# A macaron FFN turned to token-major products with 512 moving features

## The chip, the cores and the metric

The kernel runs on one core of one Trainium2 chip. The metric is the device time of one execution in microseconds. The core has a matrix engine (TensorE, PE in the profile, with its weight loads shown apart as PEld), VectorE (DVE), ScalarE (ACT), GpSimd (POOL) and SyncE (SP). SP and POOL issue most of the DMAs, each from a queue that is worked off in order. Matmul results accumulate in PSUM, which has eight banks of 128 x 512 float32.

## The reference

One encoder block on 512 tokens of 1024 features, all in float32:

```
x = x + 1/2 * (silu(g) * u) @ W_down          g, u = halves of RMSNorm(x) @ W_gu   (FFN 1)
x = x + (sigmoid(gA)*A + sigmoid(gB)*B) @ W_out      A: conv and two RG-LRU scans, B: neighbourhood attention
x = x + 1/2 * (silu(g) * u) @ W_down          with its own weights                 (FFN 2)
```

The FFN is 2816 wide, that is 22 tiles of 128 features; W_gu is 1024 x 5632, W_down 2816 x 1024. The RMSNorm's gain is multiplied into x before the product; its factor for each token (rstd, r) is applied behind the product.

## The kernel before

**Three matmuls for one.** Float32 accuracy is reached with a faster number format: every operand is cut into a high part H and a low part L (`split`, L143: a ScalarE copy that rounds, then a VectorE subtraction), and each product is H·H + H·L + L·H, three matmuls (`mm3`, L171). A weight tile of 128 x 1024 is loaded into `wraw` by SP, split into `wh` and `wl` (four buffers of each), and used.

**Features on the partitions.** x lies with features on the 128 partitions and the 512 tokens along the free axis, eight tiles. A matmul in which the weights are stationary and x moves gives features x tokens.

**FFN, gate and up.** Some feature tiles are computed plainly (`chunk`, 24 matmuls of 512 columns for a tile of g or of u); their number is NPLAIN, 4 in FFN 1 and 0 in FFN 2. The others go two at a time through `strassen` (L294), a Strassen scheme with seven products where eight would be needed. Its 2 x 2 split runs over the two halves of the features going in, the two halves of the tokens, and g against u. The x side are sums and differences of quarters of x (`a11`, `a12`, `a22` and the forms `s1` to `s4`, built once per FFN by `make_forms`); the weight side are sums that are partly built by DMAs from POOL that add into the loaded tile (`add`, L358), partly by VectorE (`after_sum`, L362). A product (`product`, L302) is 24 matmuls with 256 tokens moving: 2 feature tiles x 4 k-tiles x 3. The order in a unit is a11, a12, s1, a22 of the unit before, s2, s4, s3. Results are copied out of PSUM by ScalarE (`p1`, `p5`, `u2`), VectorE adds to them, multiplies the gate by r (L332), ScalarE takes the Silu (L333), VectorE multiplies by u (`put`, L339). h stays in SBUF, features on the partitions.

**The beginnings.** FFN 1 begins with x and the first NLEAD = 6 weight chunks arriving in pieces: for each of the eight k-tiles six chunks x 3 matmuls are done as soon as the tile is there (L464 to L468). VectorE and ScalarE make xh, xl, the sum of squares and the forms from the same tiles meanwhile. In FFN 2 two units' a11 come first, and the sum of squares is turned into r by matmuls placed by hand between products (`late`).

**FFN, down.** Two passes over the 22 h tiles (q = 0, 1), each for four of the eight output tiles in four PSUM banks; every h tile is split in each pass. The last DTAIL = 3 pairs of h are done bank by bank, so that outputs leave one after another. An output is scaled by -0.5 r (L545) and added to x (L642 in FFN 1, L1130 in FFN 2). `out1` also prepares the next stage's xh, xl and sum of squares. The last tile of the kernel is finished in two token halves over the last EHALF = 5 tiles.

**Order of work.** The program is written in one sequence; the framework's planner puts each engine's instructions in an order from priorities (program order, raised by `high_priority`), a model of durations and free buffers. `after` adds an order without a wait, and `hold` (L251) places an instruction behind the last matmul written so far.

**Token-major elsewhere.** The qkv projection (`tok_group`, L831 to L833) has slices of x stationary and 512 weight columns moving, so that its results have tokens on the partitions.

Of the kernel before, what the change touches and what calls it, by code (L numbers as in the profile page):

```python
# [16 lines left out]
P = 128  # L17
# [32 lines left out]
NLEAD = 6  # L50


NPLAIN = 4, 0
# [3 lines left out]
EHALF = 5  # L57
# [34 lines left out]
def block_kernel(ctx: ExitStack, tc, a, out):  # L92
# [19 lines left out]
    NBIG = 43  # L112
# [181 lines left out]
    def strassen(src, units, A, r, hs, ahead, late=None):  # L294

        half = T // 2
        prev = {}

        line, in_line = [], late is not None
        view = lambda t: t.rearrange("p (m t) -> p m t", m=2)  # L300

        def product(ps, w, form, first, last):  # L302
            H, L = w
            for m in range(2):
                o = ps[:, m * half : (m + 1) * half]
                for k in range(4):
                    c = slice((m * 4 + k) * P, (m * 4 + k + 1) * P)
                    xh_, xl_ = A[form][k]


                    for w_, x_ in ((H, xh_), (H, xl_), (L, xh_)):
                        mm = nc.tensor.matmul(  # L312
                            o, w_[:, c], x_, start=first and m + k == 0 and w_ is H and x_ is xh_,
                            stop=m + k == 4 and w_ is L, skip_group_check=True)
                        if line:
                            after(mm, line.pop())
            if in_line:
                line.append(mm)

        def operand(raw, form=None):  # L320

            w = hl_t()
            with tc.high_priority():
                lo = split(raw, *w)
            if form is not None:
                after(lo, mark["cut", form])
            return w

        def gate(t, tok):
            rr = r[:, tok].unsqueeze(1).to_broadcast([P, 2, half])  # L330
            s_ = big_t(n="s")
            nc.vector.tensor_tensor(view(s_), view(t), rr, ALU.mult)  # L332
            nc.scalar.activation(s_, s_, AF.Silu)  # L333
            return s_

        def put(u, s_, t, tok):
            for m in range(2):
                c = slice(m * half, (m + 1) * half)
                mark["h"] = nc.vector.tensor_tensor(hs[u * 2 + m][:, tok], s_[:, c], t[:, c], ALU.mult)  # L339

        def last_product(p):
            product(p["Z"], p["w"](), "a22", False, True)
            put(p["u"], gate(p["Z"], slice(half, T)), p["u7"], slice(half, T))

        def begin(u):

            a_ = raw_t()
            nc.sync.dma_start(a_, src[u, 0])
            Z = acc_t()
            product(Z, operand(a_), "a11", True, False)  # L350
            p1 = big_t(n="p1")
            with tc.high_priority():
                nc.scalar.activation(p1, Z, AF.Copy)
            return a_, Z, p1

        def add(u, t, i):
            with tc.high_priority():
                nc.gpsimd.dma_start(t, src[u, i], accum_op=ALU.add)  # L358

        def after_sum(t, o, form=None):  # L360
            with tc.high_priority():
                i = nc.vector.tensor_tensor(t, t, o, ALU.add)  # L362
            if form is not None:
                after(i, mark["cut", "s1"])
            return operand(t, form)

        def behind(u, form):
            return form if late is not None and u == 0 else None

        begun = {u: begin(u) for u in range(2)} if late is not None else {}  # L370
        first = set(begun)
        for u in range(units):
            a_, Z, p1 = begun.pop(u) if u in begun else begin(u)


            b_ = raw_t()
            d = pair_t().rearrange("p a b -> p (a b)")
            c = pair_t().rearrange("p a b -> p (a b)")
            in_line = late is not None and u < 2
            soon = u == 0 or u in first  # L380
            if soon:
                add(u, a_, 1)
            for t, i in ((d, 1), (b_, 3), (c, 2)):
                nc.sync.dma_start(t, src[u, i])
            X, Y = acc_t(), aux_t()
            hs += [big_t(n="h") for _ in range(2)]
            last = u == units - 1

            def gate1():
                product(Y, w_c, "a12", True, True)  # L390
                nc.vector.tensor_tensor(p1, p1, Y, ALU.add)
                return None if u == 0 and late is not None else gate(p1, slice(0, half))

            w_c = operand(c)
            if not last:
                s1 = gate1()
            w = operand(a_) if soon else after_sum(a_, d)
            add(u, d, 3)
            product(X, w, "s1", True, False)
            p5 = big_t(n="p5")  # L400
            nc.scalar.activation(p5, X, AF.Copy)
            if prev:
                last_product(prev)
            w = after_sum(a_, b_, behind(u, "s2"))
            add(u, a_, 2)
            product(Z, w, "s2", False, False)
            u2 = big_t(n="u2")
            nc.scalar.activation(u2, Z, AF.Copy)
            if u == 0 and late is not None:
                rcol = late[0](line[-1])  # L410
            product(X, operand(b_, behind(u, "s4")), "s4", False, True)
            nc.vector.tensor_tensor(u2, u2, X, ALU.add)
            product(Z, operand(d, behind(u, "s3")), "s3", False, False)
            nc.vector.tensor_tensor(p5, p5, Z, ALU.add)
            if u == 0 and late is not None:
                late[1](rcol, line[-1])
                s1 = gate(p1, slice(0, half))
            if last:
                ahead()
                s1 = gate1()  # L420
            put(len(hs) // 2 - 1, s1, u2, slice(0, half))
            prev = dict(u=len(hs) // 2 - 1, Z=Z, u7=p5, w=lambda a_=a_: operand(a_))
        last_product(prev)

    def ffn(wgu, ws, wd, xh, xl, S, ssum, plain, res, emit_out, lead=None, end=None):
        hs = []
        r = None
        pre = {}
        if lead is not None:


            for i in range(NLEAD):
                pre[i] = acc_t() if i < 3 else aux_t()
            wts = [[None] * 2 for _ in range(NLEAD)]
            for k in range(KT):
# [25 lines left out]
                if k == KT - 1:  # L461
                    r = rstd(ssum, True)[0]
# [4 lines left out]
                for i in range(NLEAD):  # L467
                    nc.tensor.matmul(pre[i], w[i][2][:, s], xh[k], start=False, stop=k == KT - 1)  # L468
# [10 lines left out]
        for m in range(plain):  # L479
            pg = chunk(2 * m)  # L480
            if r is None:
                r = rstd(ssum)[0]
# [4 lines left out]
            nc.scalar.activation(s, g, AF.Silu)  # L487
            h = big_t(n="h")
# [23 lines left out]
        for q in range(2):  # L512
# [19 lines left out]
            for j in range(FT // 2):  # L532
                ws_.append(load_w(wd[q, j], 1024))
                ahead(q * FT + 2 * j + 2 + AHEAD)
                if j < FT // 2 - DTAIL:
                    for k in (2 * j, 2 * j + 1):
                        for i in range(4):
                            put_in(i, k)
# [675 lines left out]
```

## Time and profile before

| | |
|---|---|
| median of three runs (range) | 1108.18 us (1106.54 to 1108.5) |
| the profiled execution, its span | 1106.08 us, 1104.3 us |
| TensorE busy | 1097.9 us, 99% |
| VectorE, ScalarE busy | 74%, 52% |
| moved by DMA | 175.83 MB, 159 GB/s on average |

FFN 1 fills roughly the first 351 us, the mixer the time to 758 us, FFN 2 the rest. "Busy" of TensorE counts the time in which any matmul is under way; since matmuls overlap (a 512-column one shows 0.39 us from start to end), their cost is read from the distance between starts. In a row of instructions the numbers behind the bar are busy time in us and mean duration in ns, then the idle time of the engine before them and what ended it.

### The profile page before, as it was taken

Reading aid. Unit: us, or ns where it says so; the run is one execution under the profiler, and the core shown is the slowest. Engines: PE = TensorE matmul, PEld = TensorE weight load, DVE = VectorE, ACT = ScalarE, POOL = GpSimd, SP = SyncE. Lnnn points to the kernel's source line nnn. Section 1 sums busy time; section 2 is a strip of 40 time slices with the busy share of each in tenths; the row PEclk is TensorE's granted clock in tenths of the full one; section 3 lists DMA queues with packets and bytes.
Section 4 is the critical chain, followed back from the end, with each engine's and each line's share of the span. In section 5 each row is a group of like instructions: output and inputs, shape, how many; then the busy total and the mean of one; then the engine's idle time right before and its main releaser. Section 6 shows DMA issues by size and latency. Waiting matters only on the chain.

```text
span 1104.3 us, 17667 instructions
## 1 busy us (share of the span) xinstructions
PE 1097.9 (99%) x6811; PEld 972.1 (88%) x6811; DVE 812.9 (74%) x1295; ACT 579.4 (52%) x872; POOL 141.1 (13%) x243
## 2 busy tenths in 40 slices
PE   9999999999999999999999999999999999999998
PEld 7899999988888778788887888889999999998887
DVE  7877777794745686999878995759877777785542
ACT  8554544464443678876454552356645454464330
POOL 0000000000000351231335231000000000000000
PEclk9999999999999999999999999999999999999999
DMA  8566656643423585583787674477666666553421
GB/s 269 155 170 153 149 157 162 163 153 96 134 81 105 157 249 162 155 221 102 231 241 205 184 212 142 138 219 169 184 166 146 163 170 147 150 165 96 134 77 38
DMA packets 59429, 175.83 MB, mean 159 GB/s; under 512 B 9169, under 2 KB 12753, under 8 KB 59345
## 3 DMA queue, kind: packets, MB, share of 16 engines
q1 hardware_dynamic: 43136, 127.75, 35.3%
q0 software_dynamic: 15632, 46.70, 21.1%
q8 instruction: 53, 0.87, 0.3%
q10 hardware_dynamic: 576, 0.26, 0.1%
q14 instruction: 32, 0.25, 0.1%
HBM read 150.53 MB, written 15.73 MB: 151 GB/s over the span
## 4 chain that ended last, share of the span: by engine, by line
PE 99%; DVE 0%; issue 0%
PE acc L312 31%; PE acc L172 11%; PE acc L173 11%; PE acc L174 10%; PE aux L312 5%; PE acc L831 4%; PE acc L833 4%; PE acc L832 4%; PE aux L174 4%; PE aux L173 4%; PE aux L172 4%; PE aux L1013 1%; PE aux L742 1%; PE aux L950 1%; PE acc L464 1%; PE aux L464 1%
## 5 line engine op out<-in xcount | busy, mean ns | idle before, releaser
L145 ACT ACTIVATE wh<-wraw 128x1024 fp32r<-128x1024 f32 (+3 forms) x224 | 220.4, 987 | 300.9 <-issue 94.0
L148 DVE TENSOR_TENSOR wl<-wraw,wh 128x1024 fp32r<-128x1024 f32 (+3 forms) x236 | 267.1, 1136 | 100.1 <-ACT wh L145 99.0
L312 PE MATMUL acc<-s,wh 128*128 128x256 f32 x1280 | 232.2, 283 | 0.0
L312 PEld LDWEIGHTS acc<-s,wh 128*128 128x128 f32 x1280 | 199.7, 192 | 0.0
L312 PE MATMUL acc<-s,wl 128*128 128x256 f32 x640 | 181.2, 283 | 0.0
L312 PEld LDWEIGHTS acc<-s,wl 128*128 128x128 f32 x640 | 122.9, 192 | 0.0
L172 PE MATMUL acc<-xh,wh 128*128 128x512 f32 x272 | 107.5, 395 | 0.0
L173 PE MATMUL acc<-xl,wh 128*128 128x512 f32 x272 | 106.4, 391 | 0.0
L174 PE MATMUL acc<-xh,wl 128*128 128x512 f32 x272 | 106.4, 391 | 0.0
L312 PE MATMUL acc<-xl,wh 128*128 128x256 f32 x320 | 90.6, 283 | 0.0
L312 PE MATMUL acc<-xh,wl 128*128 128x256 f32 x320 | 90.6, 283 | 0.0
L312 PE MATMUL acc<-xh,wh 128*128 128x256 f32 x320 | 90.6, 283 | 0.0
L831 PE MATMUL acc<-wh,xh 128*128 128x512 f32 x192 | 75.7, 394 | 0.0
L832 PE MATMUL acc<-wh,xl 128*128 128x512 f32 x192 | 74.8, 390 | 0.0
L833 PE MATMUL acc<-wl,xh 128*128 128x512 f32 x192 | 74.8, 389 | 0.0
L148 DVE TENSOR_TENSOR hl<-h,hh 128x512 fp32r<-128x512 f32 x88 | 57.2, 686 | 21.7 <-PE aux L173 21.4
L172 PE MATMUL aux<-hh,wh 128*128 128x512 f32 (+1 forms) x181 | 69.9, 386 | 0.0
L173 PE MATMUL aux<-hl,wh 128*128 128x512 f32 (+1 forms) x181 | 69.9, 386 | 0.0
L174 PE MATMUL aux<-hh,wl 128*128 128x512 f32 (+1 forms) x181 | 69.9, 386 | 0.0
L173 PE MATMUL acc<-hl,wh 128*128 128x512 f32 (+1 forms) x176 | 68.0, 386 | 0.0
L172 PE MATMUL acc<-hh,wh 128*128 128x512 f32 (+1 forms) x176 | 68.0, 386 | 0.0
L174 PE MATMUL acc<-hh,wl 128*128 128x512 f32 (+1 forms) x176 | 68.0, 386 | 0.0
(221 smaller groups left out, 2286.9 us busy)
## 6 DMA issues: line engine op xcount, KB each, us to landing
wraw<-wqkv SPq DMA_DIRECT2D x24, 512.0 KB, 4.3
wraw<-wg SPq DMA_DIRECT2D x24, 512.0 KB, 8.9
wraw<-w1d SPq DMA_DIRECT2D x22, 512.0 KB, 3.6
wraw<-w2s SPq DMA_DIRECT2D x22, 512.0 KB
pair<-w2s SPq DMA_DIRECT2D x22, 512.0 KB, 4.4
wraw<-w2d SPq DMA_DIRECT2D x22, 512.0 KB, 3.7
wraw<-w1s SPq DMA_DIRECT2D x18, 512.0 KB, 3.4
pair<-w1s SPq DMA_DIRECT2D x18, 512.0 KB, 4.5
```

Source lines behind the costliest of these rows:

```text
L145: nc.scalar.activation(H, raw, AF.Copy)
L148: return nc.vector.tensor_tensor(L, raw, H.bitcast(F32), ALU.subtract)
L172: nc.tensor.matmul(ps, wh, xh, start=first, stop=False, skip_group_check=skip)
L173: nc.tensor.matmul(ps, wh, xl, start=False, stop=False, skip_group_check=skip)
L174: mark["mm"] = nc.tensor.matmul(ps, wl, xh, start=False, stop=last, skip_group_check=skip)
L312: mm = nc.tensor.matmul(o, w_[:, c], x_, start=first and m + k == 0 and w_ is H and x_ is xh_, stop=m + k == 4 and w_ is L, skip_group_che ...
L464: nc.tensor.matmul(pre[i], w[i][1][:, s], xh[k], start=k == 0, stop=False)
L742: prev, mm = mm, nc.tensor.matmul(ps[d][b], W[w][o, c], X[x][o], start=x == 1, stop=w + x == 0)
L831: nc.tensor.matmul(pss[j], xh[kk][:, tj], H[:, s], start=kk == 0, stop=False)
L832: nc.tensor.matmul(pss[j], xl[kk][:, tj], H[:, s], start=False, stop=False)
L833: mark["mm"] = nc.tensor.matmul(pss[j], xh[kk][:, tj], L[:, s], start=False, stop=kk == KT - 1)
L950: mm = hold(nc.tensor.matmul(ps[hp][:, cs], q_[o, n * P : (n + 1) * P], keys(k_[o]), start=k_ is kl, stop=q_ is ql))
```

## The change

Four tiles of g and u form a unit (five units in each FFN), and NPLAIN becomes 2, 2, NLEAD 4. In a product the x side is now stationary and the weights move, 512 features at a time: two token blocks x 4 k-tiles x 3 = 24 matmuls of 512 columns, on two PSUM banks. The weight tiles come in two halves (kp), which are summed and split just before they are used. Results have tokens on the partitions, so r is a number per partition and enters through the Silu's scale and a scalar operand. h is then turned: VectorE transposes 32 x 32 blocks, SP writes the result to a buffer in memory (`hd`), and POOL's queue reads it back with rearranged addresses (`fetch`), which gives features on the partitions. The down projection is one pass over 22 tiles with eight banks: the first DFIRST = 3 tiles two banks at a time, then all eight banks for each tile, then the last DTAIL = 3 bank by bank. The -0.5 moves into the addition to x; r is already in h. The hand-placed `late` work is dropped, FFN 2 starts with its four plain chunks, and some tiles change pools (NBIG 43 to 42, the LRU's cuts go to the PT pool).

```diff
-NLEAD = 6
-NPLAIN = 4, 0
+NLEAD = 4
+NPLAIN = 2, 2
 DTAIL = 3
-EHALF = 5
+DFIRST = 3
...
+    def strassen(src, units, A, rcol, hd):
...
+        def product(pss, ws, form, first, last):
+            for kp in range(2):
+                H, L = ws[kp]() if callable(ws[kp]) else ws[kp]
+                for k2 in range(2):
+                    k = kp * 2 + k2
+                    c = slice(k2 * T, (k2 + 1) * T)
                     xh_, xl_ = A[form][k]
+                    for tb in range(2):
+                        s = slice(tb * P, (tb + 1) * P)
+                        for x_, w_ in ((xh_, H), (xl_, H), (xh_, L)):
+                            mark["mm"] = nc.tensor.matmul(
+                                pss[tb], x_[:, s], w_[:, c], start=first and k == 0 and x_ is xh_ and w_ is H,
+                                stop=k == 3 and w_ is L, skip_group_check=True)
+            flush()
...
+        def gate(ts, th):
+            ss = [big_t(n="s") for _ in ts]
+            for tb, (s_, t) in enumerate(zip(ss, ts)):
+                j = th * 2 + tb
+                nc.scalar.activation(s_, t, AF.Silu, scale=rcol[:, j : j + 1])
+            return ss
+
+        def flush():
+            while out:
+                nc_dma, t2 = out.pop(0)
+                hold(nc.sync.dma_start(nc_dma, t2))
+
+        def put(u, ss, ts, th):
+            for tb, (s_, t) in enumerate(zip(ss, ts)):
+                j = th * 2 + tb
+                mark["h"] = nc.vector.scalar_tensor_tensor(t, t, rcol[:, j : j + 1], s_, ALU.mult, ALU.mult)
+                t2 = big_t(n="ht")
+                nc.vector.transpose(
+                    t2.rearrange("p (c f i) -> p f c i", c=NCB, i=32), t.rearrange("p (f c i) -> p f c i", c=NCB, i=32))
+                out.append((hd[u][j], t2.rearrange("p (c x) -> p c x", c=NCB)))
...
         for u in range(units):
+            a_ = raws(u, 0, "pair", 4)
+            c_ = raws(u, 2, "PT", 5)
+            d_ = raws(u, 1, "PT", 5)
+            b_ = raws(u, 3, "wraw", 3)
+            Z = [acc_t() for _ in range(2)]
+            product(Z, operands(a_), "a11", True, False)
+            p1 = evict(Z, "p1")
+            if u == 0:
                 add(u, a_, 1)
...
+        def fetch(u):
+            for th in range(2):
+                t = big.tile([P, 8, NCB, 32], F32, tag="PT", bufs=5, name=nm("hT"))
+                for c in range(NCB):
+                    hold(nc.gpsimd.dma_start(
+                        t[c * 32 : (c + 1) * 32].rearrange("p g f i -> p g (f i)"),
+                        hd[u].rearrange("t (a i) c x -> c i (t a) x", a=NCB)[c][:, th * 8 : th * 8 + 8]))
+                turned[u, th] = t
...
+        for g in range(4):
+            outs = range(2 * g, 2 * g + 2)
+            for m in outs:
+                ps[m] = (aux_t, acc_t)[g % 2]()
+            for k in first:
+                for m in outs:
+                    put_in(m, k)
+        for k in range(DFIRST, FT):
+            ws_[k] = load_w(wd[k], 1024)
+            ahead(k + 1 + AHEAD)
+            if k < FT - DTAIL:
+                for m in range(KT):
+                    put_in(m, k, FT - 1 - DTAIL if end is not None and m == KT - 1 else FT - 1)
...
+        for m in range(KT):
+            if end is not None and m == KT - 1:
+                break
+            for k in range(FT - DTAIL, FT):
+                put_in(m, k)
+            emit_out(m, ps[m])
...
-        nc.vector.tensor_tensor(xres[m], ps, xres[m], ALU.add)
+        nc.vector.scalar_tensor_tensor(xres[m], ps, -0.5, xres[m], ALU.mult, ALU.add)
```

More of the change, by code (lines that the diff above doesn't have):

```diff
@@ L371, in strassen @@
-        first = set(begun)
-        for u in range(units):
[L373 to L381, printed above, removed]
-                add(u, a_, 1)
[L383 to L398, printed above, removed]
+                split(raw, *w)
@@ L409, in strassen @@
[L409 to L420, printed above, removed]
```

255 lines of the change are left out of this document (121 added, 134 removed).

## The prediction

> **What bounds the kernel now.** I read the page first: its first part for the engines, its fourth for the chain that ended last.
>
> ```profile
> span 1104.3 us, 17667 instructions
> PE 1097.9 (99%) x6811; PEld 972.1 (88%) x6811; DVE 812.9 (74%) x1295; ACT 579.4 (52%) x872; POOL 141.1 (13%) x243
> ...
> PEclk9999999999999999999999999999999999999999
> ...
> PE 99%; DVE 0%; issue 0%
> ```
>
> TensorE is busy from end to end at its full clock, and the chain is TensorE alone: a microsecond is won only by a shorter stream of matmuls, and lost wherever that stream now has to wait. A busy PE can still hide a slow pace, so I next read the chain in order of time, in which a piece of n matmuls lasts n times the distance from start to start. First the gate-and-up products of FFN 1, then the qkv projection, then the opening.
>
> ```profile
> 73.44 17.28 PE acc L312 x144
> ...
> 471.84 0.23 PE acc L831
> ...
> 480.00 0.23 PE acc L831
> ...
> 13.60 0.68 PE acc L464 x3
> ...
> 17.68 0.68 PE acc L464 x3
> ```
>
> In L312 a 256-column matmul starts every 17.28/144 = 120.0 ns. L831 to L833 are already what the change makes of L312, x stationary and 512 weight columns moving: from 471.84 to 480.00 there are 36 of them, 8.16/36 = 226.7 ns. Two narrow ones cost 240.0, one wide one 226.7. The opening spends 4.08 us on each 128 rows of x (18 wide matmuls), also without a gap.
>
> Last I looked at how near the other engines are to the end of their slack, by stretches (PE, PEld, DVE, ACT, POOL, clock, DMA): opening, seven products of FFN 1, down projection of FFN 1, and the start of FFN 2.
>
> ```profile
> 0.00:32.45 32.45, 31.39 (x136) 25.97 (x137) 25.53 (x59) 25.20 (x46) 2.68 (x12) 1.00 0.84 270
> 72.00:232.00 160.00, 160.00 (x1335) 159.96 (x1334) 121.70 (x146) 80.94 (x100) 12.81 (x15) 1.00 0.64 161
> 232.00:330.00 98.00, 98.00 (x434) 81.15 (x433) 61.99 (x104) 47.38 (x70) 0.00 (x0) 1.00 0.35 109
> 760.00:780.00 20.00, 20.00 (x170) 20.00 (x169) 18.09 (x26) 14.45 (x21) 1.70 (x2) 1.00 0.65 178
> ```
>
> VectorE is the second engine: 76% in the products, 79% in the opening, 90% where FFN 2 starts.
>
> **Seven products, 512 wide.** Before: 9 + 11 units of two feature tiles, each 7 x 24 matmuls, 3360 in all at 120.0 ns = 403.2 us. After: 5 + 5 units of four tiles, 1680 at 226.7 ns = 380.8 us. Gain 22.4 us. The plain tiles go from 4 + 0 to 2 + 2, the same number at the same width, so they add nothing.
>
> By the Trainium skill, "TensorE: Matmul & The Clock Gate", section on the 56 ns gap, back-to-back matmuls start N cycles of 2.4 GHz plus about 2.5 ns apart. Then a pair would save only 2.5 ns and the whole 4.2 us. The trace does not agree: 120.0 and 226.7 are 13.3 ns above N/2.4 in both widths, so the pairing saves 13.3, not 2.5.
>
> **VectorE and ScalarE beside it.** The rows of 72 to 232 us (eight units, that is four of the new size), and the nearest rows for what is new:
>
> ```profile
> L148 DVE TENSOR_TENSOR wl<-wraw,wh 128x1024 fp32r<-128x1024 f32 x41 | 50.1, 1222 | 14.8 <-ACT wh L145 14.8
> L148 DVE TENSOR_TENSOR wl<-pair,wh 128x1024 fp32r<-128x1024 f32 x15 | 18.3, 1222 | 9.2 <-ACT wh L145 9.2
> L362 DVE TENSOR_TENSOR wraw<-wraw,wraw 128x1024 f32<-128x1024 f32 x7 | 8.5, 1220 | 0.0
> L339 DVE TENSOR_TENSOR h<-s,u 128x256 f32<-128x256 f32 x16 | 6.7, 423 | 0.2
> L332 DVE TENSOR_TENSOR s<-acc,rstd 128x512 f32<-128x512 f32 x8 | 5.5, 692 | 5.1 <-PE acc L312 5.1
> L391 DVE TENSOR_TENSOR p<-p,aux 128x512 f32<-128x512 f32 x8 | 5.5, 688 | 5.4 <-PE aux L312 5.4
> ...
> L992 DVE STREAM_TRANSPOSE pt<-p 128x512 f32<-128x512 f32 x16 | 10.9, 684 | 0.0
> ...
> L856 DVE TENSOR_SCALAR v<-acc,rcol 128x512 f32<-128x512 f32 x8 | 5.8, 746 | 0.1
> ```
>
> Per four tiles before: 14 splits x 1.22 + 4 sums x 1.22 + 6 adds x 0.69 + 4 scalings by rstd x 0.69 + 8 half products x 0.42 = 32.2 us of 40.3. After: splits, sums and adds the same (26.1); the scaling goes into the Silu's per-row scale on ScalarE; four products with a per-row scalar (0.75, the L856 row) and four 32x32 transposes (0.68): 31.8 us of 38.1, 83%. ScalarE keeps its instructions. Four weight buffers still hold two products, 10.9 us, ahead of TensorE, so I price this at nothing; if VectorE runs out of cover it is the third rival.
>
> **h through memory.** A unit adds four writes of 256 KB on SP's queue, each behind its transpose and placed after the following product's last matmul, and eight reads of 128 KB (512-byte pieces) on POOL's queue, placed after the last product. Nearest rows, issue by issue with the median time to landing:
>
> ```profile
> PT<-pd POOLq DMA_DIRECT2D x64, 112.0 KB, 4.1
> ...
> wraw<-w1s POOLq DMA_DIRECT2D x10, 512.0 KB, 5.8
> ...
> xd<-pair SPq DMA_DIRECT2D x16, 256.0 KB, 2.3
> ```
>
> About 1 MB more per 38.1 us is 27 GB/s on top of the products' 161, which the faster pace makes 170; 270 were moved in the opening. SP's next weight loads stand behind those writes, but the transposes end about 4 us after their product and the write's place is a product (5.44 us) later. The reads stand behind the accumulating loads, the last of which leaves after s2 of the last unit, three products (16.3 us) before the down projection. Unit 0 of h is then there in time; units 1 to 4 are fetched four k-steps (21.8 us) before use. Nothing, unless the hand-over below is late.
>
> **Hand-over from products to down projection (twice).** The down projection now starts with k = 0, 1 (plain tiles) and 2 (unit 0). The cut of k = 2 stands in VectorE's queue behind the last unit's last gate: two Silu (1.2), two products and two transposes (2.9), then the cut in halves (1.2 with ScalarE's half): about 5.5 us after the last product. Its first pair of banks needs it after 12 matmuls, 2.7 us. If the planner lets the next pairs' k = 0, 1 go first, nothing waits; if not, 2.8 us. I take 0.75 each time, 1.5 in all (0 to 5.6).
>
> **Down projection.** As many matmuls. Per k-step of 24 x 226.7 ns = 5.44 us VectorE has one split and two half cuts, 1.22 + 0.84; each h is cut once, not twice. Cheaper beside the path, zero on it. At the end of FFN 1 the eight outputs come 2.04 us apart (three k-steps a bank), where four came 4.08 apart:
>
> ```profile
> 347.51 0.69 DVE L545 SCALAR_TENSOR_TENSOR dn<-acc,rstd 128x512 f32<-128x512 f32 x1 [0.52 <-PE acc L174]
> 348.23 0.69 DVE L642 TENSOR_TENSOR pair<-dn,pair 128x512 f32<-128x512 f32 x1
> ...
> 349.76 0.75 DVE L197 SCALAR_TENSOR_TENSOR xl<-pair,small,xh 128x512 fp32r<-128x512 f32 x1 [0.19 <-ACT xh L196]
> 350.43 0.69 DVE L206 TENSOR_TENSOR ssum<-ssum,xsq 128x512 f32<-128x512 f32 x1
> ```
>
> One of the first two goes, so an output costs VectorE 0.7 + 0.7 + 0.7 = 2.1 us: it just keeps pace. The mixer's first chunk needs x's last tile 21 matmuls (4.8 us) after the last output; a backlog of two outputs would make that late. I take 0.5 (0 to 3).
>
> **The opening of FFN 1.** Here cover goes. With four early chunks instead of six TensorE wants a new 128 rows every 12 x 0.2267 = 2.72 us, while x's part of the work on VectorE and ScalarE is unchanged. VectorE's rows up to the last xl (31.79 + 0.75):
>
> ```profile
> 31.79 0.75 DVE L197 SCALAR_TENSOR_TENSOR xl<-pair,small,xh 128x512 fp32r<-128x512 f32 x1
> ...
> L148 DVE TENSOR_TENSOR wl<-wraw,wh 128x512 fp32r<-128x512 f32 x6 | 3.7, 684 | 0.0
> L148 DVE TENSOR_TENSOR wl<-wraw,wh 128x1024 fp32r<-128x1024 f32 x3 | 3.7, 1221 | 0.0
> L148 DVE TENSOR_TENSOR wl<-wraw,wh 128x256 fp32r<-128x256 f32 x6 | 2.3, 419 | 0.1
> ```
>
> Of 25.5 us busy, a third of the six lead weights' rows goes (3.3 of 10.0, with the smaller pieces) and the three 1024-wide splits (3.7); 6.9 us are idle, mostly before the first data. 18.5 + 6.9 = 25.4 us, plus up to four urgent splits for a11 and a12 (4.9): 25.4 to 30.3. TensorE wants that tile at 4.8 + 7 x 2.72 + 0.9 = 24.8. So it waits 0.6 to 5.5 us. After that, s1's forms and weights, the late rows and the two plain gates, some 14 us of VectorE, stand against the 13.5 us up to s1: another 0 to 2. ScalarE (25.2 busy) and the DMAs (4.2 MB at 270 GB/s, 15.5 us) are close behind. I take 4.5 (0.6 to 9). FFN 2 gets the reverse: four plain chunks, 21.8 us, come between the mixer and the products where VectorE was at 90%; zero (0 to 2, its first chunk needing all of x).
>
> **The tail.** After the last matmul one VectorE instruction stands where there were two:
>
> ```profile
> 1100.80 0.42 DVE L558 SCALAR_TENSOR_TENSOR dn<-aux,rstd 128x256 f32<-128x256 f32 x1 [0.37 <-PE aux L174]
> 1101.26 0.42 DVE L570 TENSOR_TENSOR o<-o,dn 128x256 f32<-128x256 f32 x1
> ```
>
> It gives 0.46, and six split pairs fewer (5 halved k-steps become 3) give 6 x 13.3 ns = 0.1.
>
> **Sum.** -22.4 - 0.5 + 1.5 + 0.5 + 4.5 = -16.4 us. The profiled execution took 1106.1 us (span 1104.3 and 1.8 around it), which gives 1089.7; the runs' median, 1108.2, lies 2.1 higher, so I say 1090.5. With no stall anywhere it is 1083.2; with every stall at its upper end (5.6 + 3 + 9 + 2) 1102.8.
>
> **Rivals.**
> *The skill's gap.* Wide matmuls gain almost nothing: what is 13.3 ns a matmul would then belong to something that widening keeps. The sum is without the 22.4: 1106.1 + 6.5 - 0.5 = 1112 with nothing gained at all. Against it stand the 36 matmuls at L831. By the page named above it would be 1107.9. Chance 0.03.
> *The joins cost much more than I think:* opening, hand-overs and outputs wait 13 us together instead of 6.5, since weights, x and VectorE's order arrive late one after another. 1096, still faster. For it: the opening's 79% on VectorE with a third of the cover gone. Chance 0.17.
> *VectorE becomes the bound of the products, and the change loses.* In the quoted window it was idle 9.8 us per four tiles, nearly all in waits (14.8 + 9.2 for ScalarE's half of a split, the rest for TensorE). If those waits stay, 31.8 + 9.8 = 41.6 us a unit against 38.1: 3.5 x 10 units = 35 us, giving 1125. It decides from 1.6 us of TensorE waiting a unit, which eats the 16.4. Against it: those waits are of an engine that is ahead, and TensorE was never late under them. The same place would show a late weight load in SP's longer queue. Chance 0.12.
> *No measurable effect,* for instance with the reads of h late at each of the eight later units (2 us each): 1106. Chance 0.05.
>
> **Chances.** My forecast, 1083 to 1095, has 0.63. I count a change under 0.2% (2.2 us) as none, about what a measurement of this kernel can tell. Faster 0.63 + 0.17 = 0.80; same 0.05 with a part of the first rival, 0.06; slower 0.14. The range that leaves out the third rival runs from 1082 to 1103.
>
> **What would show it.** The product line with 1680 matmuls of 128x512 and 2.72 us per 12 in the chain: right; 240 ns: wrong. VectorE about 83% in the products with no TensorE idle there; TensorE idle in the first 40 us of 4 to 5 us, before the matmuls on x's last tiles; gaps under 3 us where the down projections begin. Idle TensorE time inside the units, or waits of VectorE's h cuts for DMAs, would make the prediction wrong.

## The result, and the profile after

The changed kernel is slower: median 1124.51 us (1122.84 to 1125.71) against 1107.92 us (1106.54 to 1108.5) for the kernel before, ratio 1.0151 with the interval 1.0131 to 1.0170. The forecast was 1090.5 us, a gain. The profiled execution took 1125.71 us, its span is 1123.9 us.

First the page of the changed kernel (span, busy time of the engines, granted clock in 40 slices, the chain that ended last by engine).

```profile
span 1123.9 us, 14418 instructions
...
PE 1089.7 (97%) x5125; PEld 892.5 (79%) x5125; DVE 773.3 (69%) x1228; ACT 561.5 (50%) x864; POOL 189.8 (17%) x324
...
PEclk9799999989999999999999999999999999989999
...
PE 89%; DVE 4%; DMA 3%; ACT 2%; issue 1%; SPq 0%; ACTq 0%; DVEq 0%
```

Before, TensorE stood at 99% in the chain and its clock at 9 in every slice. Now about a tenth of the chain belongs to other engines and to DMAs, and the clock falls in three slices: the second, the ninth and the 36th of 28.1 us each. A piece of the chain in order of time (start, length, what) shows that the products themselves are not to blame:

```profile
74.74 10.88 PE acc L322 x48
```

10.88/48 is 226.7 ns a matmul of 512 columns, exactly the pace forecast. The windows (PE, PEld, DVE, ACT, POOL busy, clock, DMA share, GB/s) put the loss in place, first of the changed kernel, then, for the first and third, of the kernel before:

```profile
0.00:60.00 60.00, 46.17 (x182) 37.97 (x183) 43.69 (x82) 37.79 (x63) 6.29 (x16) 0.87 0.81 246
60.00:230.00 170.00, 170.00 (x749) 140.68 (x749) 129.69 (x138) 89.22 (x106) 25.56 (x36) 1.00 0.68 177
230.00:260.00 30.00, 21.27 (x82) 16.30 (x81) 19.44 (x54) 11.60 (x22) 5.81 (x10) 0.83 0.72 216
980.00:1010.00 30.00, 24.61 (x96) 19.21 (x95) 18.24 (x28) 10.05 (x17) 8.72 (x16) 0.89 0.79 239
```

```profile
0.00:60.00 60.00, 58.95 (x302) 50.52 (x303) 47.16 (x93) 41.48 (x71) 3.54 (x13) 1.00 0.71 212
230.00:260.00 30.00, 30.00 (x141) 25.15 (x140) 23.24 (x56) 17.75 (x27) 0.00 (x0) 1.00 0.38 122
```

Inside the units (60 to 230 us) TensorE is never idle and VectorE is at 129.69/170 = 76%. Nearly all is lost at three joins: the opening of FFN 1 and the two changes from products to down projection. TensorE's rows that begin behind a wait (in brackets the idle time and what ended it), and two of the rows behind the longest of them:

```profile
38.06 1.84 PE L220 MATMUL aux<-ones,ssum 128*128 128x1 f32 x8 [4.95 <-DVE ssum L206]
43.28 1.09 PE L237 MATMUL aux<-ident,rcol 128*128 128x128 f32 x4 [3.38 <-DVE rcol L231]
55.70 1.22 PE L322 MATMUL aux<-wh,s 128*128 128x512 f32 x2 [4.44 <-DVE g L479]
...
246.91 0.79 PE L172 MATMUL aux<-hh,wh 128*128 128x512 f32 x1 [8.50 <-ACT wh L145]
...
249.19 0.63 PE L173 MATMUL aux<-hl,wh 128*128 128x512 f32 x1
249.62 0.63 PE L174 MATMUL aux<-hh,wl 128*128 128x512 f32 x1
...
996.41 0.79 PE L172 MATMUL aux<-hh,wh 128*128 128x512 f32 x1 [3.22 <-ACT hh L145]
998.56 0.79 PE L173 MATMUL aux<-hl,wh 128*128 128x512 f32 x1 [1.35 <-DVE hl L148]
```

Two losses, then. One is the wait. Taken over all of TensorE's starts in the trace, the part of each distance above 0.45 us that exceeds 0.227 adds up to 34.4 us, before to 2.0: 14.3 in the opening, 10.2 at the first join, 6.6 at the second, 3.3 elsewhere. The other follows the wait: from 249.19 to 249.62 a matmul takes 0.43 us, not 0.227. 38 matmuls of the trace start so far apart (before: one), which is 37 x 0.20 = 7.4 us more; 34 of the 38 stand where the trace shows a granted clock of 0.50, 32 of them in the opening and at the two joins. With the shorter stream, -22.4 - 0.5 + 32.4 + 7.4 = +16.9 of the 19.6 us between the two spans; the last 2.7 I did not trace.

The Trainium skill, "TensorE: Matmul & The Clock Gate", section on the clock gate, says that TensorE's clock is halved after about 3.4 us without work and comes back after about as long a time of work. The rows at 249 us, twice as far apart behind 8.5 us of waiting, agree with that.

**What the first join waits for.** SyncE's queue, then GpSimd's, VectorE and ScalarE of the changed kernel around 238 us:

```profile
230.51 10.98 SPq L369 DMA_DIRECT2D hd<-ht  x4
241.54 12.69 SPq L163 DMA_DIRECT2D wraw<-w1d  x7
```

```profile
214.08 3.75 POOL L502 DMA_DIRECT2D hT<-hd  x6
219.53 4.72 POOL L502 DMA_DIRECT2D hT<-hd  x8 [1.71 <-issue]
```

```profile
239.84 1.30 DVE L376 STREAM_TRANSPOSE ht<-p 128x512 f32<-128x512 f32 x2
```

```profile
237.78 1.37 ACT L363 ACTIVATE s<-acc,rcol 128x512 f32<-128x512 f32 x2 [9.84 <-PE acc L322]
...
245.80 1.06 ACT L145 ACTIVATE wh<-wraw 128x1024 fp32r<-128x1024 f32 x1 [3.68 <-DMA wraw<-w1d]
```

TensorE's last product ends at 238. The last two writes of h stand in SyncE's queue and wait for the last two transposes (to 241.1), which wait for the gate (237.78). The first down weights are *behind* these writes: issued at 241.54, split from 245.80, used at 246.91. Unit 0 of h was not late: its eight reads, the first of this queue's reads of h, are issued from 214.08 to 220.11, and such a read lands 5.0 us after its issue in the median (page, DMA issues). In FFN 2 the same queue holds the writes between the loads, and on ScalarE a split that waits for a load stands ahead of the gate and of the cuts.

**What the opening waits for.** GpSimd's queue, ScalarE and VectorE:

```profile
23.80 1.08 POOL L339 DMA_DIRECT2D pair<-w1s  x1 [22.40 <-DVE s L263]
```

```profile
32.52 1.06 ACT L145 ACTIVATE wh<-pair 128x1024 fp32r<-128x1024 f32 x1 [6.58 <-DMA pair<-w1s]
33.49 0.61 ACT L205 ACTIVATE xsq<-pair 128x512 f32<-128x512 f32 x1
```

```profile
37.23 0.69 DVE L206 TENSOR_TENSOR ssum<-ssum,xsq 128x512 f32<-128x512 f32 x1
...
54.96 0.68 DVE L479 TENSOR_TENSOR g<-aux,rstd 128x512 f32<-128x512 f32 x1
```

The transfer that adds to the weights of s1 is issued at 23.80; the split that waits for it begins 8.7 us later. This split is urgent, so it is the next in ScalarE's queue, and the last square of x (33.49) stands behind it though x is there. So the sum of squares is late (37.23), and TensorE, in whose order the matmuls of 1/rms stand ahead of a12, waits twice. Then s1 waits for PSUM banks that the plain features hold until their gate (54.96).

### The profile page after: what moved, and what is told of

It reads as the page before. It is cut to its first block, busy times and chain, and to the rows that moved or that the text cites. A ratio compares the mean times of both kernels' runs of the same rounds, so it can differ in the third digit from the quotient of the medians.

```text
span 1123.9 us, 14418 instructions
## 1 busy us (share of the span) xinstructions
PE 1089.7 (97%) x5125; PEld 892.5 (79%) x5125; DVE 773.3 (69%) x1228; ACT 561.5 (50%) x864; POOL 189.8 (17%) x324
## 4 chain that ended last, share of the span: by engine, by line
PE 89%; DVE 4%; DMA 3%; ACT 2%; issue 1%; SPq 0%; ACTq 0%; DVEq 0%
PE acc L322 18%; PE aux L322 15%; PE acc L172 10%; PE acc L173 10%; PE acc L174 10%; PE acc L851 4%; PE aux L173 4%; PE aux L174 4%; PE aux L172 4%; PE acc L852 4%; PE acc L853 4%; PE aux L1033 1%; PE aux L762 1%; DVE wl L148 1%; ACT wh L145 1%
## 5 line engine op out<-in xcount | busy, mean ns | idle before, releaser
L148 DVE TENSOR_TENSOR wl<-wraw,wh 128x1024 fp32r<-128x1024 f32 (+3 forms) x152 | 169.3, 1117 | 172.5 <-ACT wh L145 171.9
L145 ACT ACTIVATE wh<-wraw 128x1024 fp32r<-128x1024 f32 (+3 forms) x140 | 135.0, 970 | 229.3 <-PE acc L173 169.5
L148 DVE TENSOR_TENSOR wl<-pair,wh 128x1024 fp32r<-128x1024 f32 x80 | 97.7, 1222 | 49.1 <-ACT wh L145 49.1
L145 ACT ACTIVATE wh<-pair 128x1024 fp32r<-128x1024 f32 x80 | 85.0, 1062 | 83.2 <-PE aux L322 57.7
L173 PE MATMUL acc<-xl,wh 128*128 128x512 f32 x288 | 112.7, 391 | 0.0
L322 PE MATMUL aux<-wh,s 128*128 128x512 f32 x320 | 100.4, 396 | 4.4 <-DVE g L479 4.4
L322 PE MATMUL acc<-wh,s 128*128 128x512 f32 x320 | 98.5, 389 | 0.0
L322 PEld LDWEIGHTS aux<-wh,s 128*128 128x128 f32 x320 | 61.2, 192 | 17.7 <-DVE g L479 4.9
L173 PE MATMUL aux<-hl,wh 128*128 128x512 f32 (+1 forms) x179 | 71.2, 398 | 1.4 <-DVE hl L148 1.4
L322 PEld LDWEIGHTS acc<-wh,s 128*128 128x128 f32 x320 | 60.1, 188 | 12.5
L173 PE MATMUL acc<-hl,wh 128*128 128x512 f32 (+1 forms) x176 | 68.2, 387 | 0.0
L172 PEld LDWEIGHTS acc<-xh,wh 128*128 128x128 f32 x288 | 54.4, 189 | 13.0 <-issue 2.3
L174 PEld LDWEIGHTS acc<-xh,wl 128*128 128x128 f32 x288 | 54.2, 188 | 11.6 <-issue 0.4
```

Of the source, the lines that this page charges most:

```text
L145: nc.scalar.activation(H, raw, AF.Copy)
L148: return nc.vector.tensor_tensor(L, raw, H.bitcast(F32), ALU.subtract)
L172: nc.tensor.matmul(ps, wh, xh, start=first, stop=False, skip_group_check=skip)
L173: nc.tensor.matmul(ps, wh, xl, start=False, stop=False, skip_group_check=skip)
L174: mark["mm"] = nc.tensor.matmul(ps, wl, xh, start=False, stop=last, skip_group_check=skip)
L322: mark["mm"] = nc.tensor.matmul(pss[tb], x_[:, s], w_[:, c], start=first and k == 0 and x_ is xh_ and w_ is H, stop=k == 3 and w_ is L, sk ...
```

## The experiments

Two questions: is the width of the products worth what was forecast, and are the joins lost to the order in the queues, or to work that is really too much? Each kernel's median stands beside that of the changed kernel (1124.5) and its ratio is to the kernel before. The kernel before was run again with every group of experiments and had medians from 1106.6 to 1108.1 us, so a difference between medians of two groups is uncertain by 1 to 2 us.

### The width: w1_two_halves

```diff
+                            for hf in range(2):
+                                q = slice(hf * half, (hf + 1) * half)
+                                mark["mm"] = nc.tensor.matmul(
+                                    pss[tb][:, q], x_[:, s], w_[:, c][:, q],
...
```

> The changed kernel with each 512-column matmul of the seven products issued as two of 256 columns with the same stationary tile: everything else of the change is kept. If the width alone is worth 13.3 ns a pair, 1680 pairs add 22.4 us: 1146 to 1148 us. If most of the products' gain came from elsewhere, or other work hides it, less than 15 us more: under 1140.

Measured: 1143.38 us, ratio 1.0322 (1.0307 to 1.0338), 18.9 us above the changed kernel. The chain in order of time:

```profile
75.32 11.52 PE acc L324 x96
```

11.52/96 = 120.0 ns for a matmul of half the width. Over a product, 48 halves take 5.76 us, 24 whole ones 5.44. The gain per pair, 13.3 ns, is real. The time rises less than 1680 x 13.3 = 22.4 us, and less than expected; summed as above, the waits of this kernel are 30.1 us instead of 34.4, about as much as is missing.

### The first join: h1_loads_first, h2_loads_cuts_first, h3_writes_behind_loads

h1: the first three loads of down weights ahead of the last two writes of h.

```diff
-        flush()
         ps = [None] * KT
...
+        for k in first:
+            ws_[k] = load_w(wd[k], 1024)
+        flush()
```

> The changed kernel with one edit: the loads of the first three down weights of each FFN stand on SP's queue ahead of the last two writes of h, not behind them. Queue theory (the down projection starts late because its first weights wait on SP behind writes that wait for the last transposes): the weights land near 236 us, the 8.9 us gap of TensorE before the first down matmul falls to the 3 to 4 us that the cuts of the plain h tiles, behind the transposes on VectorE, still take; with the half-clock stretch behind a long gap gone too, about 1113 to 1117 us. Rival (the down projection waits for h itself, through memory, or for VectorE's backlog): the gap stays above 7 us and the time at 1122 to 1126.

Measured: 1120.40 us, ratio 1.0118 (1.0099 to 1.0138); a gain of 4.1 us, about half of what was expected or less. TensorE at the first join:

```profile
241.49 0.61 PE L172 MATMUL aux<-hh,wh 128*128 128x512 f32 x1 [3.19 <-ACT hh L145]
244.41 0.79 PE L173 MATMUL aux<-hl,wh 128*128 128x512 f32 x1 [2.31 <-DVE hl L148]
```

The weights are there, now the cuts of the *plain* features are late, ready since the opening but behind the last gate and transposes. h2 makes those cuts within the last unit:

```diff
+            if u == units - 1:
+                early()          # ahead(plain)
```

> The edit of h1_loads_first, and the two plain h tiles are cut in the last unit of the products, not after it. Queue theory: nothing that the first matmuls of the down projection need stands behind the last unit's transposes; the gap falls under 1.5 us in both FFNs and the time to 1105 to 1110 us. Rival (VectorE has no time for it): within 2 us of h1_loads_first.

Measured: 1116.43 us, ratio 1.0080 (1.0065 to 1.0095). Better by 4.0 us, and short of the forecast again: the gap at 238 us is gone and another stands 16 us later, at the fourth feature. TensorE, and ScalarE before it:

```profile
253.71 0.73 PE L172 MATMUL aux<-hh,wh 128*128 128x512 f32 x2 [3.86 <-ACT hh L145]
```

```profile
252.29 1.06 ACT L145 ACTIVATE wh<-wraw 128x1024 fp32r<-128x1024 f32 x1 [0.72 <-DMA wraw<-w1d]
253.25 2.55 ACT L145 ACTIVATE hh<-hT 128x256 fp32r<-128x256 f32 x8
```

The weights of the later features are now the ones behind the writes, and the cuts of h stand behind their splits. h3 puts the two writes behind six loads:

```diff
+            if k == DFIRST + 2:
+                flush()
```

> As h2_loads_cuts_first, and the last two writes of h in each FFN stand behind the first six loads of down weights in SyncE's queue instead of the first three (h of that unit is fetched only some eight features later). Theory (the 4.25 us gap at 249.5 us of h2_loads_cuts_first is the weights of features 3 to 5, held in SyncE's queue behind the two writes, whose splits then hold the cuts of h on ScalarE): that gap falls under 1 us, FFN 2's two gaps of 1.9 and 1.4 us fall with it, and the time falls by 5 to 9 us to 1107 to 1112 us. Rival (the cuts of h wait for the fetch of h from memory by GpSimd's queue, not for the splits ahead of them): a gap of 3 us or more stays at the same place, with the cut's end on the fetch, and the time stays above 1114.

Measured: 1114.89 us, ratio 1.0066 (1.0052 to 1.0080). Neither theory holds whole: not the loads alone, and not the fetch of h. TensorE, ScalarE and VectorE:

```profile
251.76 0.50 PE L172 MATMUL aux<-hh,wh 128*128 128x512 f32 x1 [1.91 <-ACT hh L145]
254.58 0.67 PE L173 MATMUL aux<-hl,wh 128*128 128x512 f32 x1 [2.32 <-DVE hl L148]
```

```profile
248.35 1.06 ACT L145 ACTIVATE wh<-wraw 128x1024 fp32r<-128x1024 f32 x1 [1.36 <-PE acc L173]
```

```profile
253.89 0.17 DVE L692 TENSOR_SCALAR pol<-pol 128x16 f32<-128x16 f32 x1
254.10 1.43 DVE L148 TENSOR_TENSOR hl<-hT,hh 128x256 fp32r<-128x256 f32 x4
```

The split at 248.35 waits for one of four weight buffers, which come free only when TensorE is done with the first three features (the release is L173). The cuts of h, whose data is there, stand behind it. On VectorE a cut stands behind `pol`, a chain of small steps for the mixer's decay, each waiting for the one before.

### h4_cuts_before_weights and h5_polynomial_back

```diff
+                with tc.high_priority():
+                    cut(k)
...
+            for e, d in zip(("act", "dve"), done[min(k + 1, FT - 1)]):
+                after(mark[e], d)
...
-    after(nc.vector.tensor_scalar(nlam, lam, -1.0, None, ALU.mult), mark["h"])
+    after(nc.vector.tensor_scalar(nlam, lam, -1.0, None, ALU.mult), mark["mid"])
```

h4 is h3 with three edits: the cuts of h are urgent, each later feature's weights are split behind the cuts of the feature after it, and the polynomial starts in the middle of the down projection (`mark["mid"]` is the last matmul ahead of feature 12).

> As h3_writes_behind_loads, with the cuts of h as urgent as the weights' splits and each later feature's weights split behind the cuts of the feature after it, and the small polynomial of the mixer's decay moved from the start to the middle of the down projection. Theory (the 4.9 us left at 249.5 us are cuts of h that stand behind splits which wait for a weight buffer held until the first three features are done, and on VectorE behind the polynomial): no gap above 1 us is left at either hand-over, and the time falls by 6 to 10 us against h3_writes_behind_loads, to 1105 to 1109 us. Rival (h fetched from memory, the GpSimd queue's transfers, is late by itself): a gap of 2 us or more stays with its end on a transfer of h, and the time stays above 1111.

Measured: 1104.86 us, ratio 0.9981 (0.9971 to 0.9990): 10.0 us under h3, 19.6 under the changed kernel (18.8 by the two ratios), with not one wait of TensorE over 1 us left at either join. h5 is h4 without the last of the three edits:

> As h4_cuts_before_weights, with the mixer's small polynomial back where the changed kernel has it, right behind the last gate of FFN 1. What is told apart: whether the order of the cuts and weights alone, or also the 18 small steps on VectorE, held the cuts of h at the first hand-over. If the polynomial counts by itself, 1 to 3 us come back at the first hand-over only (a gap between 238 and 256 us whose end is on VectorE) and the time is 1 to 4 us above h4; if the cuts' order alone decides, no gap comes back and the time is within 1 us of 1104.9.

Measured: 1107.83 us, ratio 1.0006 (0.9996 to 1.0015), 3.0 us above h4 (2.8 by the two ratios). At the joins a single wait comes back, its end on VectorE. VectorE, then TensorE:

```profile
250.60 0.17 DVE L705 TENSOR_SCALAR sn<-sp 128x16 f32<-128x16 f32 x1
250.72 0.76 DVE L148 TENSOR_TENSOR hl<-hT,hh 128x256 fp32r<-128x256 f32 x2
```

```profile
251.20 0.50 PE L174 MATMUL aux<-hl,wh 128*128 128x512 f32 x1 [1.81 <-DVE hl L148]
...
252.06 0.63 PE L174 MATMUL aux<-hl,wh 128*128 128x512 f32 x1
252.49 0.63 PE L175 MATMUL aux<-hh,wl 128*128 128x512 f32 x1
```

So the rest of h3's loss was both: the polynomial for 3 us and, by difference, the order of cuts and weights for 7; the polynomial's edit was not run without the other two.

### The opening: o1_sum_unit0, o2_x_before_weights, o5_order_by_need

o1: in unit 0 VectorE makes s1's weight sums, as in every later unit.

```diff
-            if u == 0:
-                add(u, a_, 1)
...
-            w = operands(a_) if u == 0 else sums(a_, d_)
+            w = sums(a_, d_)
```

> The changed kernel with one edit: in unit 0 the weights of s1 are summed by VectorE from two loaded tiles, as in all later units, not by a DMA that adds into the first tile. Theory (the opening loses 14 us of gaps because ScalarE's next split stands in its queue waiting 6.6 us for that adding DMA, with the last square of x, and so rstd, behind it): the gaps of 5.3 and 3.7 us before the rstd matmuls shrink to 1 to 2 us, the last one, where s1 waits for PSUM banks of the plain tiles, comes earlier by as much; 1112 to 1118 us. Rival (VectorE's load in the opening is too high, my prediction's reason): two more sums of 1.2 us make it worse by 2 us, 1125 to 1128.

Measured: 1117.25 us, ratio 1.0091 (1.0074 to 1.0107), 7.3 us less. The waits on 1/rms are gone and one of 6 us is there. VectorE, then TensorE:

```profile
35.19 1.23 DVE L344 TENSOR_TENSOR pair<-pair,wraw 128x1024 f32<-128x1024 f32 x1
...
36.99 0.76 DVE L197 SCALAR_TENSOR_TENSOR xl<-pair,small,xh 128x512 fp32r<-128x512 f32 x1
```

```profile
37.80 0.79 PE L458 MATMUL acc<-xl,wh 128*128 128x512 f32 x1 [6.02 <-DVE xl L197]
```

Urgent weight sums, some of them for the product after next, overtake x's last tile. o2 takes the urgency from a12's and s1's weights in unit 0:

> As o1_sum_unit0, and in FFN 1's unit 0 the splits of the second and third products' weights (a12 and s1) and the sum for s1 lose their urgency, so that x's last tile, its squares and 1/rms stand ahead of them on ScalarE and VectorE. Theory (the two opening gaps of o1_sum_unit0, 6.4 us before x's last tile and 2.2 us before s1, are urgent weight work that overtook the work on x): the first gap falls under 1.5 us, TensorE's half-speed stretch behind it goes too, and the time falls by 4 to 8 us against o1_sum_unit0, to 1109 to 1113 us. Rival (the work on x is itself late: the seven forms' differences and casts fill VectorE up to there): the gaps stay above 6 us together and the time stays within 2 us of 1117.

Measured: 1117.98 us, ratio 1.0092 (1.0076 to 1.0107): no gain. The wait before x's last tile went, as the theory said, and TensorE stood still later for longer. VectorE, then TensorE:

```profile
44.47 1.22 DVE L348 TENSOR_TENSOR pair<-pair,wraw 128x1024 f32<-128x1024 f32 x1
...
49.44 0.68 DVE L481 TENSOR_TENSOR g<-aux,rstd 128x512 f32<-128x512 f32 x1
```

```profile
50.27 1.19 PE L323 MATMUL aux<-wh,s 128*128 128x512 f32 x2 [10.27 <-DVE g L481]
```

Now the gate `g`, which frees the PSUM banks that s1 wants, comes last, behind the sums for s2 and the cuts of the four forms s1 to s4 (the expectations speak of seven). o5 goes back to the adding transfer and orders the opening by need:

```diff
+            if u == 0 and lead is not None and "r" in mark:
+                after(mark["act"], mark["r"])
...
-                pre[i] = acc_t() if i < 2 else aux_t()
+                pre[i] = aux_t() if i < 2 else acc_t()
...
-        (lead, one, lead_step, lambda: (forms.finish(), forms.finish())))
+        (lead, one, lead_step, lambda: (forms.cut("s1"), forms.cut("s1")),
+         lambda: [forms.cut("s2") for _ in range(2)], lambda: [forms.cut(n) for n in FORMS[2:] for _ in range(2)]))
```

Sums and splits of unit 0 also lose their urgency. Only s1 is cut ahead of the plain gates, s2 behind them, s4 and s3 before their products; s1's weights are split behind the copy of 1/rms (`mark["r"]`).

> The changed kernel with only the opening of FFN 1 put in the order of need: the adding transfer of unit 0 stays, but its sums and splits lose their urgency, the split of s1's weights stands behind the copy of 1/rms on ScalarE, only s1 of the seven forms is cut ahead of the gates of the plain features (s2 behind them, s4 and s3 before their products), and the first plain feature's results stand in the second set of PSUM banks, which s1's product takes next. Theory (the opening lost 14.3 us to work that stood in its engine's queue ahead of work needed sooner: first urgent weight work ahead of x, then, with that undone, casts of late forms ahead of the gates that free PSUM): less than 4 us of gaps are left before 60 us, TensorE runs no matmul there at half its clock, and the time is 11 to 16 us under the changed kernel's, 1109 to 1114 us. Rival (VectorE has simply too much work there: sums, splits, forms and gates for the first three products): the gap moves again and stays above 8 us, 1117 to 1123 us.

Measured: 1109.87 us, ratio 1.0026 (1.0016 to 1.0036), 14.6 us less (13.8 by the two ratios). Two waits, 0.92 and 1.26 us, are what is left before 60 us. The rival, too much work for VectorE, falls with it: not one instruction of the work was taken away. What each of o5's edits is worth alone was not measured.

### Together: c1_all, c2_order_everywhere, c3_order_and_halves

c1 is o2 and h3 together:

> Both together: opening of o2_x_before_weights and hand-over of h3_writes_behind_loads. The width of the products stays. Theory (the whole loss lies at the opening and at the two hand-overs; units, mixer and end gain 22 us): 1088 to 1102 us, faster than before. Rival (a part of the loss is elsewhere, in the lanes through memory that the units set up, so that the gaps only move): above 1106, no faster than before.

Measured: 1109.84 us, ratio 1.0020 (1.0011 to 1.0029), outside the range and above the 1106 of the rival: it keeps the waits of both, above all the 10 us before s1, so it cannot tell whether the loss is elsewhere. c2 is o5 and h4 together:

> Both together, nothing else. Theory (all that the change lost it lost to order in the queues at the opening and the two hand-overs, and the half clock behind those gaps): 1088 to 1097 us, a ratio of 0.983 to 0.991 to the kernel before. Rival (some of the loss is in the moved work itself): 1100 or more.

Measured: 1089.37 us (1088.55 to 1090.68), ratio 0.9843 (0.9829 to 0.9858). The gains of the two, 14.6 and 19.6, add up: 34.2 against 35.1 (by the ratios 32.6 against 34.1). It beats both kernels. The page of c2, and its windows at the opening and the first join:

```profile
span 1088.2 us, 14419 instructions
...
PE 1078.0 (99%) x5125; PEld 883.3 (81%) x5125; DVE 772.8 (71%) x1228; ACT 559.5 (51%) x864; POOL 189.0 (17%) x324
...
PEclk9999999999999999999999999999999999999999
```

```profile
0.00:60.00 60.00, 56.18 (x244) 44.86 (x245) 49.85 (x88) 44.25 (x72) 6.27 (x16) 1.00 0.92 281
215.00:245.00 30.00, 29.34 (x129) 23.65 (x128) 20.91 (x37) 14.28 (x29) 6.44 (x12) 1.00 0.88 264
```

VectorE and ScalarE do the same work (772.8 and 559.5 us, against 773.3 and 561.5); the clock is whole again in all 40 slices. c3 is c2 with each matmul of the products in two halves:

> As c2_order_everywhere, with each matmul of the products issued as two of half the width (256 columns), as the kernel before had them; all else stays. If the width is worth what the rows say once nothing waits (120.0 ns per 256 columns against 226.7 ns per 512, 13.3 ns over 1680 matmuls is 22.3 us), the time rises by 19 to 23 us to 1108 to 1113 us, the time of the kernel before or a little above it. If much of the gain of c2 came from the new order alone, beyond undoing the loss, it stays under 1100.

Measured: 1115.64 us, ratio 1.0073 (1.0056 to 1.0090), 26.3 us above c2 (25.5 by the two ratios) and so about 3 us more than expected. FFN 2's units alone, from the first start of a product to the last, take 202.21 us against 191.21: 11.0 for 840 matmuls, 13.1 ns each, as forecast. In FFN 1 they take 13.9 us more. The clock explains the rest: c3's trace shows two stretches of 3.41 us at clock 0.50, from 57.38 us (it makes the 0.93 of the window from 40 to 60 us, where c2 has 1.00) and, in the mixer, from 613.75 us; c2 has none before its last matmul. Half of 6.83 is 3.4 us, and 22.4 + 3.4 = 25.8 us is the difference of the two spans, 1114.0 and 1088.2.

```profile
40.00:60.00 20.00, 16.47 (x124) 15.86 (x123) 16.00 (x20) 14.17 (x21) 1.72 (x2) 0.93 0.83 251
```

The gain of c2 is the width's, not the order's: without the width the reordered kernel is no faster than the kernel before.

## Why the prediction was wrong

**Right.** The width: 226.7 ns, 22.4 us over all products, shown by the chain and by both kernels with halves. The first rival, that wide matmuls gain next to nothing, is out, and with it the 2.5 ns gap that the Trainium skill, "TensorE: Matmul & The Clock Gate", gives in its section on the 56 ns gap. VectorE in the products: 76% where 83% was worked out (the same working gives 32.2/40.3 = 80% for the kernel before, whose window shows 76%, so it counts some 4 points too many), and no wait of TensorE in the units, so the third rival, to which nearly all of "slower" was given, is out too. That its 1125 us lies on the measured time is a coincidence: the slowdown came from elsewhere. And the sum for a kernel without misplaced work was near: 1089.7 us for the profiled execution, 1090.01 in c2, though partly by luck, since the terms below were meant to be in it.

**The hand-over term (1.5 us, 0 to 5.6) failed in cause and size.** It named the cut of feature 2 behind the last gate on VectorE. The first wait was for weights: SyncE's two writes of h, waiting for the transposes, with the weight loads behind them. The step that let this through is in "h through memory": it names the loads behind those writes, and dismisses them because "the write's place is a product (5.44 us) later". That is true inside the units. Behind the last product no further product follows, and just there the next loads are the urgent ones. The term measured 10.2 and 6.6 us of waits (starts against starts) and, behind them, 16 matmuls at half clock, 3.2 us; h4 takes 19.6 us away. Of the named cause only what stood behind that wait was found: the cuts of the plain features behind the gate (h1, h2), the cuts of h behind splits (h3, h4).

**The opening (4.5 us, 0.6 to 9) failed likewise.** That VectorE would be late with x's last tile showed only once, in o1, for a reason that was half in the working: it had urgent splits ahead of that tile, but not the urgent sums. Missing were the adding transfer, 8.7 us from its issue to the urgent split that waits for it in ScalarE's queue; the place of the 1/rms matmuls ahead of a12 in TensorE's order; and the banks that the plain features hold. 14.3 us of waits and 16 slow matmuls in place of 4.5; o5 takes 14.6 us away. The working counted what each engine has to do and compared sums, and the sums were right: c2 does the same work in time. It did not ask in which order each queue would do it.

**The small terms hold as far as they can be seen.** TensorE has no wait over 0.5 us at the end of FFN 1 or in the opening of FFN 2. In the tail VectorE ends 1.19 us behind the start of the last matmul before and 0.73 in the changed kernel, the forecast 0.46 less. From there to the end of the span it is 2.62 and 2.98 us, so little of that shows in the time.

**The clock was not in the sum at all.** In the trace of the kernel before TensorE waited only once between two matmuls for more than 1 us, 1.81 us in the mixer, and no matmul behind it ran at half clock, so no row told of it. 34 x 0.20 = 6.8 us of the loss are of this kind.

**The second rival, joins that cost 13 us,** had the right place and was given 0.17; the joins cost about three times that. Its 1096 us and the range's 1103 came from taking each wait as a few us: even the upper ends together, 5.6 + 3 + 9 + 2 = 19.6 us, are about half of that. What the prediction said would prove it wrong did not fit either: the idle time was not inside the units, and what waited for a DMA at the first join was a weight, not a cut of h.

## What to carry to other kernels

Where work changes stage, write out each queue in its order across the join and look for the instruction that waits for the last result of the old stage: all that stands behind it, loads above all, is late by the whole chain from that result. Urgency given to work that waits for a transfer, or for a buffer, does the same inside an engine: it holds up ready work behind it. Undoing one such wait uncovers the next (five layers at the join here, three in the opening), so a first repair that gains half of what was forecast is a reason to read the trace again, not to drop the theory.

## What was not expected of the hardware

TensorE's clock was halved behind waits much shorter than 3.4 us: in h5_polynomial_back a single wait of 1.81 us is followed, 0.86 us after it ends, by matmuls 0.43 us apart from 252.06 to 255.41, that is for 3.35 us. In c2 waits of 0.92 and 1.28 us in the opening were followed by none. The Trainium skill, "TensorE: Matmul & The Clock Gate", section on the clock gate, gives 3.4 us of idle time as the point from which it happens; the length of the slow stretch agrees with that number, the wait before it does not.

The length of the wait alone does not decide it. A wait of 1.81 to 2.04 us for the same cut in the mixer stands in every kernel's trace, in the changed kernel so:

```profile
626.04 0.40 PE L970 MATMUL aux<-kl,qh 64*128 64x256 f32 x2 [1.81 <-DVE kl L949]
```

Here 3.41 us at clock 0.50 follow, from 627.49 us. In the kernel before and in c2 the wait is 1.81 us too, and the clock stays at 1.00 behind it; of the 14 traces five show the slow stretch there. Where the wait falls seems to count. In each trace that has several of them, the stretches at clock 0.50 begin whole multiples of 3.41 us apart. In the 3.41 us just ahead of the slow stretch TensorE was busy for 1.60 us, both in h5 (248.51 to 251.92) and in the changed kernel (624.08 to 627.49). In the kernel before the wait lies across two such slices, busy for 3.22 and 1.79 us. That a slice less than about half busy brings a slow one is read from these few slices and was not tested.

So in h5's trace the wait and what follows it cost 1.8 + 1.7 us (half of 3.41), and the medians of h5 and h4 differ by 3.0. The price of a wait should be taken with what may follow it.
